# A hybrid decoder trunk on one core: the order of the mixer stage rewritten (C's norm inside the input projection, output projection C, D, B, A, joined squares)

## The chip, the core and the metric

The kernel runs on one core of one Trainium2 chip. The metric is the device time of one execution in microseconds (us). The core has TensorE (PE in the rows; PEld is its weight load, which overlaps it), VectorE (DVE), ScalarE (ACT), GpSimd (POOL) and SyncE (SP), which here only starts transfers. Each engine works through its own instructions in program order and waits on semaphores for the others.

## What is computed

Two layers, each of three steps on the same 320 tokens (256 of a prompt, 64 of eight samples), 1024 channels:

```python
x = LN(alpha*x + 1/2*(1+g1)*SwiGLU1(mod1(x)))
x = LN(alpha*x + (1+g2)*W_out[A|B|C|D](mod2(x)))   # the mixers
x = LN(alpha*x + 1/2*(1+g3)*SwiGLU2(mod3(x)))
u, v, xb, gate_b, gate_c, hc, glu_a, glu_g = split(modulate(x, sh2, sc2) @ w_in[l])
ya = gelu(u) * (W_s @ layer_norm(gelu(v)) + b_s)            # A: 4 heads of 64 channels
yb = (causal means of 2, 4, 8, 16 of xb - xb) @ pool_w * s  # B
yc = gate_b * conv3(gate_c * hc)                            # C
yd = silu(layer_norm(conv31(glu_a * sigmoid(glu_g)) + b))   # D
mix = rms_norm_groups([ya|yb|yc|yd]) @ w_out[l]
```

The shift, scale and gate of every step come from a projection of the sequence's condition ("ada" below), whose matmuls and small operations are spread over the whole kernel. The rms norm is taken over each of the four groups of 256 channels by itself, and the output projection needs the normed group of the rows of W_out that it multiplies.

## The kernel before

**Tiles.** Activations stand transposed: a tile is 128 channels x 320 tokens, so x is eight tiles and each of A, B, C, D two. Weights come through SP's queue as raw tiles of 128 x 2048 fp32; each half (128 x 1024) is one *split*: ACT copies it to `whi` (L229, a rounded copy), DVE takes `wlo = raw - whi` (L237). Activations are split the same way, into `xhi/xlo` and, for the mixers' outputs, `mh` (ACT, L845) and `ml` (DVE, L851). A product of one 128 x 128 weight tile with a 128 x 320 tile is then three matmuls (hi*hi, hi*lo, lo*hi). `acc3` (L664 to L666) does one product at a time; `kouter` (L673, L674, L678) takes one input row k and feeds several output tiles at once.

**The mixer stage**, once in each layer, is `mix_body`. Its parts in order:

- `zchunk` multiplies the eight rows of x into five output tiles `zcm0` to `zcm4`: the two halves of D's `glu_a`, the two of its `glu_g`, and the first half of B's input. D's gate (`sigmoid`, product) follows, and then its 31-tap causal convolution: the first tap of each half on ACT (`dtap0`), the other thirty on DVE, `dtap` (L915), one instruction for one tap of one half, 60 in a layer. They are laid between the other work by `hook`, a function that is called as each weight tile of a projection is taken and issues taps while a credit is left (0.465 a tap).
- the list `MIX_SEQ` gives the order of everything else by short names; the program issues each name's instructions on whatever engines they run on, and that order is the order of every engine. `hc`, `gc`, `gb` are C's three projections for one half, `xb`, `up`, `val` those of B and A. `mean` first empties the list of taps and then computes D's channel mean (`cmn`, L1108, PE); `sub` subtracts it (L1112, DVE), `sq4` squares (ACT, L826), `stat4` sums the squares over channels (PE, `rr`, L534), `pow4` makes the inverse root (DVE L1123, POOL L1124), `bc4` spreads it over the partitions (PE, L603), `norm` and `swish` finish D. Groups 2 (C), 3 (D), 1 (B) and 0 (A) then go through `sq`, `stat`, `pow`, `bc`, `mul` (DVE L834), `hi` and `lo` the same way. `cconv`, `ctaps`, `cgate` are C's product, taps and gate on DVE. `pool` and `poolmm` are B's running sums (DVE) and its small projection (`pb`, PE L966), `sgu` and `sgate` A's mixing over tokens (`pm`, PE L1027 and L1029) and its gate. `ada` is a piece of the ada projection (`adp`, L461).
- `ko0` to `ko5` multiply the first six rows of the output projection (groups in the order `WO_GROUPS`, two rows each) into the first `CH` = 5 output tiles `wo`; the loop over `WO_ORDER` then finishes these five with the last two rows (6 matmuls each) and computes the other three whole (24 matmuls each). After each tile comes `evac`: gate, add to x (DVE L816, ACT L817, DVE L819), and `acc_add`, which keeps the running sums S and Q of x and x*x for the LN (DVE L558, L559). `TAIL_SPLIT` says after which tiles a weight split of the next stage is made.
- the LN (`ln_finish`): the last sums (L574, L575), their total over channels on PE (`nbm`, `rbm`, L534), and so on to the first product of the next stage (`zch` after the mixers).

The PSUM tiles come from a pool of six banks handed out in turn and one of two for the small statistics.

```python
MIX_SEQ = """
    pool0 hc0 xb1 up0 val vstat up1 gc0 gb0 vnorm cconv0 gc1 hc1 gb1 mean cconv1 sub sq4 ada6 ctaps0 ctaps1 cgate0
    cgate1 stat4 pow4 vgain ada2 sq2 bc4 norm swish stat2 sq3 sgu pow2 pool1 ada2 stat3 bc2 pow3 poolmm mul2 hi2
    sq1 sgate bc3 lo2 sq0 ada2 stat1 mul3 hi3 pow1 ko0 stat0 lo3 pow0 bc1 mul1 ko1 hi1 lo1 step step bc0 mul0 hi0
    ada18 ko2 lo0 ko3 ko4 ko5
"""
```

Of the kernel before, what the change touches and what calls it, by code (L numbers as in the profile page):

```python
# [61 lines left out]
WO_ORDER = (0, 1, 3, 2, 6, 5, 4, 7)  # L62
WO_GROUPS = (2, 1, 3, 0)
TAIL_SPLIT = (1, (0, 0, 0, 0, 2, 1, 0, 0))
# [7 lines left out]
""".split()
MIX_OPS = [(w.rstrip("0123456789"), int("0" + w.lstrip("abcdefghijklmnopqrstuvwxyz"))) for w in MIX_SEQ]
# [4 lines left out]
            "mul": 0.9, "lo": 0.8, "sub": 0.8, "norm": 0.8}  # L78
# [214 lines left out]
class Kern:  # L293
# [389 lines left out]
    def zchunk(self, nm, n, mid=None):  # L683
# [173 lines left out]
    def mix_body(self, l, gb, G, late):  # L857
# [32 lines left out]
        banks = self.zchunk(nm, CH, sig_table)  # L890
# [26 lines left out]
        taps = [dtap(i, j) for i in range(1, 31) for j in range(2)]  # L917
# [11 lines left out]


# [89 lines left out]
        def spatial():  # L1020
            for jj in range(2):
                pt = self.mm(f"pm{l}{jj}")
                for hh in range(2):
                    h = 2 * jj + hh
                    o = pt[64 * hh:64 * hh + 64]
                    for cc in range(2):
# [395 lines left out]
```

## Time and profile before

| | before |
|---|---|
| runs | 1307.23, 1304.6, 1293.9 us (median 1304.6) |
| the profiled execution's own time | 1306.28 us |
| its span, first to last instruction | 1304.5 us |
| PE busy | 1268.1 us (97%) |
| DVE, ACT, POOL busy | 730.3, 555.6, 23.3 us |
| matmuls | 9310 |
| mean granted TensorE clock | 0.977 |
| mixer stage, layer 0: first `zcm` to first `zch` | 286.91 to 422.03 us |
| mixer stage, layer 1 | 915.34 to 1056.93 us |

A row of the timeline has the start, the duration, the engine, the line and the operation, out<-in, how often it stands in a row, and in brackets the engine's idle time before it and who ended it. A row of several instructions gives the time from the first's start to the last's end. On PE, one fp32 matmul is counted as two or more passes, and a duration is that of one instruction in the pipeline: neighbouring ones overlap, so the step from start to start is what a matmul costs. PEclk is the granted share of the 2.4 GHz clock, 0.50 meaning 1.2 GHz.

### The profile page before, as it was taken

How to read it: one execution, taken by the hardware profiler on the slowest of the kernel's cores; microseconds unless marked ns; L12 is line 12 of the kernel's file. 1: busy time of each engine (PE TensorE's matmuls, PEld its weight loads, DVE VectorE, ACT ScalarE, POOL GpSimd, SP SyncE). 2: the span in 40 equal slices, each digit the busy share in tenths (PEclk: the TensorE clock that was granted, in tenths of full speed). 3: DMA queues.
4: the chain of work that ended last, by engine and by line, in shares of the span. 5: the costliest groups of instructions: out<-in, count | busy, mean ns of one | idle time of the engine just before them, and what ended most of it. 6: DMA issues, size and time to landing. Idle time of an engine off the chain costs nothing.

```text
span 1304.5 us, 22088 instructions
## 1 busy us (share of the span) xinstructions
PE 1268.1 (97%) x9310; PEld 1215.6 (93%) x9310; DVE 730.3 (56%) x1321; ACT 555.6 (43%) x872; POOL 23.3 (2%) x39
## 2 busy tenths in 40 slices
PE   6999999999999999999999999999997999999996
PEld 4999999999888999999999999999995989999996
DVE  4644444468966744454575444445896575444444
ACT  3643333347344634343345343333742446343432
POOL 0000000000010000000000000000000000000000
PEclk9999999999979999999999999999996999999998
DMA  9765556568849654544465546554864794444301
GB/s 375 282 236 209 211 194 248 201 215 245 303 162 120 264 204 137 205 149 162 162 218 206 181 172 216 183 206 161 227 251 162 73 262 163 134 157 157 134 1 41
DMA packets 63747, 247.45 MB, mean 190 GB/s; under 512 B 31072, under 2 KB 33632, under 8 KB 34464
## 3 DMA queue, kind: packets, MB, share of 16 engines
q1 hardware_dynamic: 58912, 245.11, 56.0%
q8 instruction: 73, 1.20, 0.4%
q10 hardware_dynamic: 4736, 0.93, 0.4%
q14 instruction: 26, 0.21, 0.1%
HBM read 243.45 MB, written 2.57 MB: 189 GB/s over the span
## 4 chain that ended last, share of the span: by engine, by line
PE 72%; issue 19%; DVE 5%; DMA 2%; ACT 1%; POOL 0%; SPq 0%; POOLq 0%; ACTq 0%; DVEq 0%
PE of L664 4%; PE of L666 4%; PE adp L461 4%; PE of L665 4%; PE uf L664 4%; PE uf L666 4%; PE uf L665 4%; PE gf L664 3%; PE gf L666 3%; PE gf L665 3%; PE oh L665 2%; PE oh L666 2%; PE oh L664 2%; DVE aD L915 2%; PE uh L664 2%
## 5 line engine op out<-in xcount | busy, mean ns | idle before, releaser
L237 DVE TENSOR_TENSOR wlo<-raw,whi 128x1024 fp32r<-128x1024 f32 x312 | 373.7, 1226 | 135.6 <-ACT whi L229 134.9
L229 ACT CAST whi<-raw 128x1024 fp32r<-128x1024 f32 x312 | 315.1, 1045 | 26.2 <-issue 8.4
L664 PE MATMUL of<-hhf,whi 128*128 128x320 f32 x352 | 109.6, 311 | 0.0
L666 PE MATMUL of<-hhf,wlo 128*128 128x320 f32 x352 | 109.1, 310 | 0.0
L665 PE MATMUL of<-hlf,whi 128*128 128x320 f32 x352 | 109.1, 310 | 0.0
L665 PE MATMUL oh<-hlh,whi 128*128 128x320 f32 x352 | 108.6, 309 | 0.0
L666 PE MATMUL oh<-hhh,wlo 128*128 128x320 f32 x352 | 108.6, 309 | 0.0
L664 PE MATMUL oh<-hhh,whi 128*128 128x320 f32 x352 | 108.6, 309 | 0.0
L664 PE MATMUL uf<-xhif,whi 128*128 128x320 f32 x320 | 99.5, 311 | 0.0
L664 PE MATMUL uh<-xhih,whi 128*128 128x320 f32 x320 | 99.1, 310 | 0.0
L665 PE MATMUL uh<-xloh,whi 128*128 128x320 f32 x320 | 99.0, 309 | 0.0
L666 PE MATMUL uf<-xhif,wlo 128*128 128x320 f32 x320 | 99.0, 309 | 0.0
L666 PE MATMUL uh<-xhih,wlo 128*128 128x320 f32 x320 | 99.0, 309 | 0.0
L665 PE MATMUL uf<-xlof,whi 128*128 128x320 f32 x320 | 99.0, 309 | 0.0
L664 PE MATMUL gf<-xhif,whi 128*128 128x320 f32 x304 | 94.6, 311 | 0.0
L664 PE MATMUL gh<-xhih,whi 128*128 128x320 f32 x304 | 94.2, 310 | 0.0
L666 PE MATMUL gf<-xhif,wlo 128*128 128x320 f32 x304 | 94.0, 309 | 0.0
L666 PE MATMUL gh<-xhih,wlo 128*128 128x320 f32 x304 | 94.0, 309 | 0.0
L665 PE MATMUL gf<-xlof,whi 128*128 128x320 f32 x304 | 94.0, 309 | 0.0
L665 PE MATMUL gh<-xloh,whi 128*128 128x320 f32 x304 | 94.0, 309 | 0.0
L767 ACT CAST hhf<-sgf 128x320 fp32r<-128x320 f32 x44 | 20.2, 459 | 134.3 <-DVE sgf L764 134.3
L767 ACT CAST hhh<-sgh 128x320 fp32r<-128x320 f32 x44 | 20.2, 459 | 134.3 <-DVE sgh L764 134.3
(332 smaller groups left out, 2818.0 us busy)
## 6 DMA issues: line engine op xcount, KB each, us to landing
raw<-in_w_main SPq DMA_DIRECT2D x156, 1024.0 KB, 4.9
raw<-in_w_ada SPq DMA_DIRECT2D x72, 1024.0 KB, 6.6
out_yT<-x SPq DMA_DIRECT2D x8, 160.0 KB, 1.8
xt<-in_x SPq DMA_DIRECT2D x2, 512.0 KB
wsT<-in_wsT SPq DMA_DIRECT2D x2, 256.0 KB
sgln<-in_sgln SPq DMA_DIRECT2D x2, 256.0 KB, 4.8
cD<-in_pre_d SPq DMA_DIRECT2D x4, 120.0 KB, 9.3
out_o_ds<-cD ACTq DMA_DIRECT2D x4, 120.0 KB, 14.0
```

The source lines that it names most:

```text
L229: kk.nc.scalar.copy(hi, raw)
L237: self.kk.nc.vector.tensor_tensor(lo, raw, hi, op=ALU.subtract)
L461: nc.tensor.matmul(ps[32 * g:32 * g + 32, 0:w], self.cs[:, k, :], wt[:, h, g * w:(g + 1) * w], start=(k == 0), stop=(k == NK - 1))
L664: mm(ps, hi, xh, start=first, stop=False)
L665: mm(ps, hi, xl, start=False, stop=False)
L666: mm(ps, lo, xh, start=False, stop=last)
L767: nc.scalar.copy(hi, sg)
L915: return lambda: V.scalar_tensor_tensor(o, cD[j][:, :, i:i + 8], wv, o, op0=ALU.mult, op1=ALU.add)
```

## The change

Everything changed lies in the mixer stage; the arithmetic is the same apart from the order of some sums.

- `MIX_SEQ` is rewritten. C's six projections come first, in the order gc, hc, gb, and C's product, taps, gate, squares, statistics, `mul`, `hi` and `lo` follow while the projections of B and A (`xb`, `val`, `up`) still run. `ko0` and `ko1`, C's two rows of the output projection, stand ahead of `mean`.
- `WO_GROUPS` goes from C, B, D, A to C, D, B, A. Four tiles, not five, are begun by rows (`CHO`). In the last loop, tiles that were begun by rows (6 matmuls left) and tiles computed whole (24 matmuls) take turns, and the weight splits are laid after other tiles (`TAIL_SPLIT`).
- `qa` adds the two squared tiles of a group on DVE, so that the sum over channels takes half the matmuls; `mean` adds the two halves of D first, likewise.
- In `zchunk` the last rows of x go tile by tile (`MIX_LAST`), the two tiles of D's half 0 first; D's half 0 is gated, and four of its taps are issued, ahead of half 1.
- B's second running sum (`pool1`) is cut into pieces (`p2`, `p3`, ...) laid between the steps of D's norm; `vgain` comes after `norm`; `w` makes one weight split; the two heads of a `pm` tile take turns.
- PSUM tiles are handed out in turn, so that the new order gives other banks: the program now has `pb00`, `pb01` and `pm01` in one bank and `adp32` and `pm00` in another, one after the other, where all six had banks of their own.

```diff
-WO_ORDER = (0, 1, 3, 2, 6, 5, 4, 7)
-WO_GROUPS = (2, 1, 3, 0)
-TAIL_SPLIT = (1, (0, 0, 0, 0, 2, 1, 0, 0))
+WO_ORDER = (0, 4, 1, 5, 2, 6, 3, 7)
+WO_GROUPS = (2, 3, 1, 0)
+CHO = 4
+TAIL_SPLIT = (1, (0, 1, 0, 1, 0, 1, 0, 0))
...
+    gc0 hc0 pool0 gb0 cconv0 gc1 hc1 ctaps0 gb1 cconv1 ctaps1 xb1 cgate0 cgate1 sq2 val qa2 stat2 pow2 up0 bc2 mul2 hi2
+    lo2 vstat up1 vnorm ko0 t99 ko1 mean p2 sub sq4 p3 ada4 qa4 stat4 p2 pow4 p4 ada4 bc4 step p9 norm swish poolmm
+    step vgain sq3 step sgu qa3 stat3 sq1 pow3 sgate bc3 mul3 hi3 qa1 stat1 lo3 pow1 sq0 ko2 bc1 mul1 hi1 qa0 lo1 stat0 ko3
+    pow0 w ko4 bc0 mul0 hi0 w ko5 lo0 w
...
+MIX_HEAD = (12, 13, 14, 15, 4)
+MIX_LAST = [(k, m) for k in (4, 5) for m in range(4)] + [(k, m) for ms in ((0, 2), (1, 3)) for m in ms for k in (6, 7)] \
+    + [(k, 4) for k in range(4, 8)]
...
-        self.qlast = (self.d0 if m == 1 else self.accS, d, self.square(d, f"{self.nm}{m}"))
+        self.qlast = (self.d0 if self.first else self.accS, d, self.square(d, f"{self.nm}{m}"))
+        self.first = False
...
+            if last and k >= 4:
+                if k == 4 and mid:
+                    mid()
+                cut = next(i for i, (kk, _) in enumerate(last) if kk > 5)
+                for kk, m in last[:cut] if k == 4 else last[cut:]:
+                    self.acc3(banks[m], st.tile(), self.xk(kk), False, kk == NK - 1)
+                continue
...
-        taps = [dtap(i, j) for i in range(1, 31) for j in range(2)]
+        taps = [dtap(i, 0) for i in range(1, 5)] + [dtap(i + 4 * (1 - j), j) for i in range(1, 27) for j in range(2)]
+        taps += [dtap(i, 1) for i in range(27, 31)]
...
+        dgate(0)
+        dtap0(0)
+        taps_(4)
+        dgate(1)
+        dtap0(1)
...
-                banks.extend(self.mm(f"wo{l}{m}") for m in range(CH))
+                banks.extend(self.mm(f"wo{l}{m}") for m in range(CHO))
...
-            for j in range(2):
-                nc.tensor.matmul(rr[5][:, 0:N], self.o256, aD[j], start=(j == 0), stop=(j == 1))
+            s = mp.tile([P, N], F32, tag="rsq", bufs=4, name=f"sD{l}")
+            V.tensor_tensor(s, aD[0], aD[1], op=ALU.add)
+            nc.tensor.matmul(rr[5][:, 0:N], self.o256, s, start=True, stop=True)
...
+        def qa(grp):
+            a, b = qs[grp]
+            V.tensor_tensor(a, a, b, op=ALU.add)
+            qs[grp] = [a]
...
+        def ahead_one(_):
+            st.split_until(min(st.nsplit + 1, ahead(st.u) + 1))
...
-            po = banks[m] if m < CH else self.mm(f"wo{l}{m}")
-            for k in range(6 if m < CH else 0, NK):
+            po = banks[m] if m < CHO else self.mm(f"wo{l}{m}")
+            for k in range(6 if m < CHO else 0, NK):
```

Three places in the order of the instructions follow. A row is line, operation, out<-in and shape; the numbers behind names tell buffers apart.

**First place: DVE ahead of D's mean, layer 0.** Before, from the last taps (`aD`) on, with the split `wlo85`, C's product `ec`, the subtraction of the mean (L1112) and C's taps (`yC`):

```order
L915 SCALAR_TENSOR_TENSOR aD00_3154<-cD00_2901,par_79,aD00_3154 128x320
L915 SCALAR_TENSOR_TENSOR aD01_3155<-cD01_2905,par_79,aD01_3155 128x320
L237 TENSOR_TENSOR wlo85_3714<-raw74_3537,whi85_3713 128x1024
L1065 TENSOR_TENSOR ec01_2920<-hc01_3676,gcs01_3674 128x256
L1066 TENSOR_TENSOR esc01_2921<-hc01_3676,gcs01_3674 128x8x8
L1112 TENSOR_TENSOR aD00_3154<-aD00_3154,cmn0_3750 128x320
L1112 TENSOR_TENSOR aD01_3155<-aD01_3155,cmn0_3750 128x320
L1080 SCALAR_TENSOR_TENSOR yC00_3610<-ec00_2912,par_79,yC00_3610 128x256
```

Of the change, from C's joined squares (L1153) to the sum of D's halves (L1141) that the mean reads:

```order
L242 TENSOR_TENSOR wlo83_3616<-raw71_3350,whi83_3615 128x1024
L1153 TENSOR_TENSOR sqrm020_3547<-sqrm020_3547,sqrm021_3549 128x320
L1162 TENSOR_SCALAR rv02_3681<-rr02_3677 128x3
...
L847 SCALAR_TENSOR_TENSOR yC00_3338<-yC00_3338,par_79,rr02_3677 128x320
...
L864 TENSOR_TENSOR ml021_3730<-yC01_3479,mh021_3729 128x320
...
L242 TENSOR_TENSOR wlo85_3747<-raw74_3513,whi85_3746 128x1024
...
L926 SCALAR_TENSOR_TENSOR aD00_3154<-cD00_2901,par_79,aD00_3154 128x320
...
L1141 TENSOR_TENSOR sD0_3819<-aD00_3154,aD01_3155 128x320
```

C's taps, gate, join, `mul` and `ml` and the split `wlo85` now all stand ahead of the last taps of D; eleven taps are left behind the join.

**Second place: PE from D's mean on, layer 0.** Before (`adp` is the ada projection, `rr` the statistics, here of D):

```order
L666 MATMUL gb01_3712<-xhim07_3068,wlo81_3525 128x320
L1108 MATMUL cmn0_3750<-aD00_3154,o256_101 128x320
L1108 MATMUL cmn0_3750<-aD01_3155,o256_101 128x320
L461 MATMUL adp32_3764<-raw75_3539,cs_78 32x256 x8
L461 MATMUL adp32_3764<-raw75_3541,cs_78 32x256 x8
```

Of the change, up to B's projection `pb` and A's mixing `pm`:

```order
L684 MATMUL wo03_3785<-ml021_3730,whi82_3554 128x320
L1142 MATMUL cmn0_3818<-sD0_3819,o256_101 128x320
L466 MATMUL adp32_3838<-raw75_3515,cs_78 32x256 x8
...
L539 MATMUL rr04_3860<-o256_101,sqrm040_3831 128x1 x3
...
L609 MATMUL rr04_3860<-ident_80,rv04_3866 128x128 x2
...
L995 MATMUL pb00_3906<-pl00_3285,pw0_2058 128x320
L995 MATMUL pb01_3909<-pl01_3822,pw0_2058 128x320
L489 MATMUL adp32_3838<-sel_81,adev14_3896 128x36 x2
```

The mean stood behind the last projection, `gb01`; now it stands behind C's two rows of the output projection, and D's statistics take one row of three where six matmuls stood.

**Third place: DVE at the end of the stage, layer 0.** Before, from the last split `wlo93` to the last tile (`evsm07`):

```order
L237 TENSOR_TENSOR wlo93_4258<-raw82_3783,whi93_4257 128x1024
L816 TENSOR_TENSOR evsm05_4263<-wo05_4232,ada0_107 128x64
L558 TENSOR_TENSOR Sm0_4114<-Sm0_4114,x6_353 128x320
L559 TENSOR_TENSOR Qm0_4115<-Qm0_4115,sqm06_4230 128x320
L819 TENSOR_TENSOR x5_239<-x5_239,evsm05_4263 128x320
L816 TENSOR_TENSOR evsm04_4277<-wo04_3965,ada0_107 128x64
L558 TENSOR_TENSOR Sm0_4114<-Sm0_4114,x5_239 128x320
L559 TENSOR_TENSOR Qm0_4115<-Qm0_4115,sqm05_4269 128x320
L819 TENSOR_TENSOR x4_237<-x4_237,evsm04_4277 128x320
L558 TENSOR_TENSOR Sm0_4114<-Sm0_4114,x4_237 128x320
L559 TENSOR_TENSOR Qm0_4115<-Qm0_4115,sqm04_4283 128x320
L811 TENSOR_TENSOR evsm07_4310<-wo07_4285,ada0_107 128x64
```

Of the change, the same stretch:

```order
L242 TENSOR_TENSOR wlo92_4245<-raw82_3857,whi92_4244 128x1024
L829 TENSOR_TENSOR evsm06_4248<-wo06_4219,ada0_107 128x64
L564 TENSOR_TENSOR Sm0_4080<-Sm0_4080,x2_233 128x320
L565 TENSOR_TENSOR Qm0_4081<-Qm0_4081,sqm02_4217 128x320
L832 TENSOR_TENSOR x6_353<-x6_353,evsm06_4248 128x320
L829 TENSOR_TENSOR evsm03_4262<-wo03_3785,ada0_107 128x64
L564 TENSOR_TENSOR Sm0_4080<-Sm0_4080,x6_353 128x320
L565 TENSOR_TENSOR Qm0_4081<-Qm0_4081,sqm06_4254 128x320
L832 TENSOR_TENSOR x3_235<-x3_235,evsm03_4262 128x320
L564 TENSOR_TENSOR Sm0_4080<-Sm0_4080,x3_235 128x320
L565 TENSOR_TENSOR Qm0_4081<-Qm0_4081,sqm03_4268 128x320
L824 TENSOR_TENSOR evsm07_4295<-wo07_4270,ada0_107 128x64
```

The split `wlo93` has left the stretch (it now stands in the LN, behind the subtraction of the mean from three tiles), and the tile before the last is a short one again, but one that the 24 matmuls of `wo06` precede.

## Rows read from the trace of the kernel before

**Rows 1.** Waits of PE: us in total, times, longest us.

```profile
PE nbm L534 <- DVE Sm L574: 5.9, 2, 3.0
```

**Rows 2.** Timeline of PE, layer 0, from D's mean to the first output row.

```profile
354.40 1.24 PE L1108 MATMUL cmn<-aD,o 128*128 128x320 f32 x4
355.56 2.80 PE L461 MATMUL adp<-raw,cs 128*32 128x256 f32 x48
358.29 1.50 PE L534 MATMUL rr<-o,sqrm 128*128 128x1 f32 x12
...
361.08 0.88 PE L603 MATMUL rr<-ident,rv 128*128 128x128 f32 x6 [0.29 <-POOL rv L1124]
...
363.18 0.65 PE L1027 MATMUL pm<-wsT,v 128*64 128x128 f32 x4
...
368.49 2.70 PE L534 MATMUL rr<-o,sqrm 128*128 128x1 f32 x12
371.05 1.52 PE L603 MATMUL rr<-ident,rv 128*128 128x128 f32 x6
372.37 2.45 PE L966 MATMUL pb<-pl,pw 128*128 128x320 f32 x4
...
378.00 0.39 PE L673 MATMUL wo<-mh,whi 128*128 128x320 f32 x1
```

**Rows 3.** Timeline of PE, layer 1, the same places and the last output row.

```profile
984.17 2.50 PE L1108 MATMUL cmn<-aD,o 128*128 128x320 f32 x4 [5.75 <-DVE aD L915]
...
1012.35 0.61 PE L673 MATMUL wo<-mh,whi 128*128 128x320 f32 x1
...
1045.23 0.31 PE L666 MATMUL wo<-mh,wlo 128*128 128x320 f32 x1
```

**Rows 4.** Timeline of DVE, layer 0, around D's mean.

```profile
352.89 0.56 DVE L915 SCALAR_TENSOR_TENSOR aD<-cD,par,aD 128x320 f32<-128x320 f32 x1
353.35 1.23 DVE L237 TENSOR_TENSOR wlo<-raw,whi 128x1024 fp32r<-128x1024 f32 x1
354.49 0.43 DVE L1065 TENSOR_TENSOR ec<-hc,gcs 128x256 f32<-128x256 f32 x1
...
355.67 0.89 DVE L1112 TENSOR_TENSOR aD<-aD,cmn 128x320 f32<-128x320 f32 x2 [0.62 <-PE cmn L1108]
356.47 0.48 DVE L1080 SCALAR_TENSOR_TENSOR yC<-ec,par,yC 128x256 f32<-128x256 f32 x1
...
358.84 0.89 DVE L1083 TENSOR_TENSOR yC<-yC,gbs 128x320 f32<-128x320 f32 x2
...
372.68 1.01 DVE L834 SCALAR_TENSOR_TENSOR yC<-yC,par,rr 128x320 f32<-128x320 f32 x2 [1.29 <-PE rr L603]
```

**Rows 5.** Timeline, PE of an FFN's LN, then PE and DVE of layer 0's mixers' end.

```profile
281.50 0.83 PE L534 MATMUL nbf<-o,Sf 128*128 128x1 f32 x6
...
286.91 0.41 PE L673 MATMUL zcm<-xhim,whi 128*128 128x320 f32 x1
...
406.95 0.31 PE L664 MATMUL wo<-mh,whi 128*128 128x320 f32 x1
...
410.32 0.31 PE L666 MATMUL wo<-mh,wlo 128*128 128x320 f32 x1
...
413.69 0.22 DVE L811 TENSOR_TENSOR evsm<-wo,ada 128x64 f32<-128x64 f32 x1
...
415.02 0.83 PE L534 MATMUL nbm<-o,Sm 128*128 128x1 f32 x6 [2.95 <-DVE Sm L574]
...
422.03 0.41 PE L673 MATMUL zch<-xhih,whi 128*128 128x320 f32 x1
```

**Rows 6.** Windows: us, busy of PE, PEld, DVE, ACT, POOL, then PEclk, DMA share, GB/s.

```profile
365.00:375.00 10.00, 10.00 (x40) 8.32 (x40) 4.69 (x18) 0.68 (x2) 0.85 (x1) 0.50 0.46 194
416.00:419.00 3.00, 3.00 (x23) 2.43 (x26) 1.46 (x7) 0.00 (x0) 0.85 (x1) 0.54 0.78 116
997.00:1016.00 19.00, 18.48 (x76) 16.16 (x75) 9.92 (x30) 6.10 (x14) 2.66 (x3) 0.50 0.21 87
```

More of the change, by code (lines that the diff above doesn't have):

```diff
@@ L77 @@
 DVE_COST = {"pool": 3.5, "vstat": 1.3, "vnorm": 0.1, "cconv": 0.5, "ctaps": 1.2, "cgate": 0.4, "vgain": 2.0, "sgate": 1.0,
-            "mul": 0.9, "lo": 0.8, "sub": 0.8, "norm": 0.8}
+            "mul": 0.9, "lo": 0.8, "sub": 0.8, "norm": 0.8, "qa": 0.4}
 def _pcols():
@@ L548, in acc_add @@
         if m == 0:
-            self.d0 = d
+            self.d0, self.first = d, True
             self.nc.scalar.activation(self.accQ, d, AF.Square)
@@ L681, in xk, with zchunk @@
         return self.xhi[k], self.xlo[k]
-    def zchunk(self, nm, n, mid=None):
+    def zchunk(self, nm, n, mid=None, last=None):
         st = self.st
@@ L888, in sig_table @@
             nc.scalar.activation(t, self.mhalf[:, 0:1], AF.Sigmoid)
-        banks = self.zchunk(nm, CH, sig_table)
+        banks = self.zchunk(nm, CH, sig_table, MIX_LAST)
         ga, gg = banks[0:2], banks[2:4]
@@ L928, in mix_body, with taps_ @@
         st.hook = hook
+        def taps_(n):
+            for _ in range(min(n, len(taps))):
+                taps.pop(0)()
+                self.credit -= DVE_TAP
         def bcopy(j, px):
@@ L1022, in spatial @@
                 pt = self.mm(f"pm{l}{jj}")
[L1023 to L1026, printed above, removed]
+                hs = [(2 * jj + hh, pt[64 * hh:64 * hh + 64]) for hh in range(2)]
+                for cc in range(2):
+                    for h, o in hs:
                         nc.tensor.matmul(o[:, cc * P:(cc + 1) * P], vb[cc][:, h * 64:(h + 1) * 64],
                                          self.wsT[:, h, :], start=True, stop=True)
+                for h, o in hs:
                     nc.tensor.matmul(o[:, NP_:N], vb[2][64:128, h * 64:(h + 1) * 64],
@@ L1160, in win @@
             return go
-        def taps_(n):
-            for _ in range(min(n, len(taps))):
-                taps.pop(0)()
-                self.credit -= DVE_TAP
-        ops = {"xb": win(lambda _: bcopy(1, self.proj(self.mm(f"xb{l}1")))), "val": win(lambda _: value()), "up": win(up),
+        def ahead_one(_):
+            st.split_until(min(st.nsplit + 1, ahead(st.u) + 1))
+        ops = {"w": ahead_one, "p": pool_part, "qa": qa, "xb": win(lambda _: bcopy(1, self.proj(self.mm(f"xb{l}1")))), "val": win(lambda _: value()), "up": win(up),
                "gc": win(cgin), "hc": win(chin), "gb": win(cbin), "vstat": lambda _: v_stat(),
@@ L1277, in _mix_tiles @@
     out = []
-    for k in range(NK):
-        out += [i[k, m] for m in (12, 13, 14, 15, 4)]
+    for k in range(4):
+        out += [i[k, m] for m in MIX_HEAD]
+    out += [i[k, MIX_HEAD[m]] for k, m in MIX_LAST]
     at = {"xb": 4, "val": 2, "up": 0, "gc": 8, "hc": 10, "gb": 6}
@@ L1286, in _mix_tiles @@
     for k in ks[:6]:
-        out += [o[k, m] for m in range(CH)]
+        out += [o[k, m] for m in range(CHO)]
     for m in WO_ORDER:
-        out += [o[k, m] for k in (ks[6:] if m < CH else ks)]
+        out += [o[k, m] for k in (ks[6:] if m < CHO else ks)]
     return out
```

44 lines of the change are left out of this document (23 added, 21 removed).

## The prediction, made before the changed kernel ran

> **What bounds the kernel now.** I read the waits first: PE is busy nearly all the time, and two waits of PE in the mixer stage stand out. The LN after the mixers waits for DVE's last sum in both layers, 5.9 us together [rows 1], and D's mean waits in layer 1 for the last tap, 5.75 us [rows 3]. Then I read PE's timeline from the mean to the first row of the output projection: 354.40 to 378.00, so 23.6 us in layer 0 [rows 2], and 984.17 to 1012.35, so 28.2 us in layer 1 [rows 3]. There PE is "busy", but with small pieces that follow the chain of D's norm, and the clock is low for a good part of it: 0.50 from 365 to 375 and from 997 to 1016 [rows 6]. The same small pieces show the price: twelve passes of a statistic take 1.50 us at one level and 2.70 at the other, spreading it 0.88 and 1.52 [rows 2]. The third view is the end of the stage: the last `wo` matmul starts at 410.32, but DVE begins the last tile's evacuation at 413.69, and `nbm` waits 2.95 us [rows 5]. So the mixer stage has three stretches that the change can move: until the mean, mean to first row of D, and the tail. Everything before and after it is unchanged, matmul for matmul.
>
> Clock, from these rows: after the 5.75 us without PE work in layer 1 the mean's four passes took 2.50 us, against 1.24 in layer 0, where PE came to it busy [rows 2, 3]; and 0.54 was granted behind the LN's wait of 2.95 [rows 5, 6].
>
> **Term 1, the mean comes later.** DVE's 60 taps set the mean. Before, the last tap of layer 0 is done at 353.4, with a split behind it [rows 4], and PE is just through with its projections at 354.4. After, DVE has ahead of the mean what it did behind it: C's taps 2.37 (eight from 356.47 to 358.84), C's gate 0.89, the second product about 0.5, `mul` 1.01, `ml` 0.9, the split 1.2 [rows 4], and two new adds, C's join and the sum of D's halves, 0.45 each by the subtraction's 0.89 for two [rows 4]. Less overlap between neighbours, that is 7.4. DVE also waits now: behind the join it needs PE's statistic (three matmuls, half of 1.50) and then, in front of `mul`, the spread root, which on PE stands behind a whole projection (24 x 0.147 = 3.5; the step 0.147 is 3.37 us over 23 steps, from 406.95 to 410.32 [rows 5]). With the root's 1.29 (358.29 + 1.50 to 361.08 [rows 2]) running beside it, and 2.9 us of taps and a split to do meanwhile, that leaves about 3.5 us of waiting in layer 0, hi and lo included. The mean then comes at 353.4 + 7.4 + 3.5 = 364.3, +10.0. PE itself would be there at about 362.7: it gets to C's statistic at 346.8 (354.4 less two projections of 3.5 and 0.5 of ada), waits for the join until 350.0, and then has the statistic 0.75, ada 0.5, two projections and 24 row matmuls (3 x 3.5) and the spread 0.88. In layer 1 DVE is the late one already, so it hardly waits for PE: 984.2 + 7.8 = 992.0. D's half 0 beginning 2.6 us earlier buys little, as DVE then still waits for half 1. Sum: **+10.0 and +7.8**. Bounds: if DVE doesn't wait for PE, +7 in layer 0; if the 3.2 us that PE waits for the join lower the clock for the next 24 matmuls (0.147 becomes 0.265 by the ratio 2.70 to 1.50), +2.8.
>
> **Term 2, from the mean to D's first row.** 24 row matmuls (3.5 us), C's statistic, spread, `mul`, `hi`, `lo` and taps are gone from here. What is left is one chain. In us from the mean at full clock: mean 0.6 (half of 1.24); subtraction, squares (passes of 0.45) to 2.1; DVE's pieces of B's sums 1.1 and the join to 3.2; statistic 0.75, to 4.0; root 1.3; the spread behind 32 ada matmuls (2.80 x 32/48 = 1.9) from 5.9 to 6.7; norm and swish to 8.6. Then the shared banks: `pb01` must wait until ACT, behind the swish, has read `pb00`, and ACT's second read stands ahead of D's squares: 0.5 + 0.6 (a quarter of 2.45 twice, at the higher clock) + 0.5, squares 0.85, to 11.2. `pm00`, `pm01` (about 0.85 a head pair, 0.65 for its four large passes [rows 2]) and the statistic to 13.1; A's gate on DVE (2.0, before `mul`) to 15.3; half of `mul` 0.5, `hi` 0.4 and semaphores: **16.7**. With statistics at 1.35, spreads at 1.52 and the mean at 1.25, the values of the lower clock [rows 2, 3], it is 19.9, and up to 22 in layer 1, where PE has idled about 5 us ahead of the mean. Before, the clock fell in this stretch [rows 6], and the stretch is as thin as it was. I take values between, nearer to the lower clock for layer 1: 18.5 and 20.5, so **-5.1 and -7.7**.
>
> **Term 3, D's first row to the last `wo` matmul.** Before: 378.00 to 410.6, 32.6 us [rows 2, 5], and 33.2 in layer 1 (1012.35 to 1045.5 [rows 3]). After: 48 + 24 + 96 = 168 matmuls of 0.147 are 24.7, spreads and a statistic 2.1; and two waits: B's statistic chain delays A's squares' join by 1.7 behind DVE's `mul` and `ml`, and A's `ml` stands behind a split whose `whi` ACT makes only after `hi`: 2.2. Together 30.7; with the first row's twelve matmuls at 0.265, 32.2; taken 31.5: **-1.1 and -1.7**.
>
> **Term 4, the tail.** With short and long tiles in turns a pair takes PE 30 x 0.147 = 4.4 us, while DVE has two evacuations with their sums (1.35 each) and at most one split: 3.9. DVE is free when the last tile ends, and the 2.95 us go. With no wait the clock has less reason to fall: an FFN's LN needs 5.4 us from first statistic to next product, this one 7.0 [rows 5], with 0.54 granted in it [rows 6]. Of these 1.6 the split moved into the LN's chain takes back up to 0.6. So **-4.0** each; bounds -2.95 (clock falls all the same) and -4.5.
>
> By the Trainium skill's "TensorE: Matmul & The Clock Gate", section "HAM oscillation — how this bites in real kernels", a gap in which TensorE waits sends it back to the low clock and the next matmuls start slow; rows 3 and 6 agree (2.50 against 1.24 behind 5.75 us of idling). By it the change buys nothing at the mean, as it keeps that wait in layer 1 and puts one of 3.2 us ahead of C's statistic in layer 0; this is the second rival's case.
>
> **Sum.** Layer 0: 10.0 - 5.1 - 1.1 - 4.0 = -0.2. Layer 1: 7.8 - 7.7 - 1.7 - 4.0 = -5.6. Together -5.8. Against the profiled execution's own 1306.28 that is 1300.5; the median of the runs shown is 1.7 lower, 1304.6, which gives 1298.8. **1299 us.** The joined squares and fewer statistics are in terms 2 and 3; the pairing of `pm`'s heads I cost at nothing (PE isn't late there, A's gate behind it is).
>
> **The rivals.** *The clock stays high* (2.4 GHz) through D's chain, since it is shorter and has ada matmuls between: term 2 is 16.7, term 3 30.7, term 4 -4.5. Layer 0: 10.0 - 6.9 - 1.9 = +1.2; layer 1: 7.8 - 11.5 - 2.5 = -6.2; less 9.0: -14.0, **1290.6**. For it: the chain loses C's pieces, which stood in the slow part. Against: the row 997 to 1016 [rows 6] behind just such a wait. Chance 0.22.
>
> *The clock stays low*, the other side: the idling ahead of the mean, or ahead of C's statistic, drops it to 1.2 GHz, and the thin chain does not bring it back before `ko5` in either layer. It decides if the 48 row matmuls of D and B run at 0.265 rather than 0.147: 48 x 0.118 = 5.7 a layer, of which 1.35 is in the 32.2 above. Layer 0 with all upper values: 10.0 + 2.8 - 3.7 + 0.4 = +9.5; layer 1: 7.8 - 6.2 - 0.2 = +1.4; 8.7 for the rows; tail -5.9: +13.7, **1318**. For it: 19 us at 0.50 in layer 1 before [rows 6]. Against: before, the output rows brought the clock back within a few us. Chance 0.08.
>
> *The tail gains nothing*, because DVE comes late again, through the split in the turns or A's late `ml`: +8, **1307**. Against: DVE's 3.9 us of work in 4.4. Chance 0.15.
>
> **How the numbers follow.** My forecast has 0.55. Its own range, by the bounds of terms 2 to 4, is 1293 to 1309 (upper values 9.5 + 1.4 - 5.9 = +5.0). The 8 in 10 reach into the first rival and take in the third: 1288 to 1311. A measurement of this kernel tells about 1% from no change, the runs of before lie 1% apart. Faster by over 1% (under 1291.6) is most of the first rival and the low end of mine: 0.23; slower by over 1% (over 1317.6) is the second: 0.07; the rest 0.70.
>
> **What would show it.** In the changed profile: the mean at about 364 and 992, behind waits of DVE's sum; first D row 18 to 21 us later; `pb01` behind ACT's `pl`; a wait at A's first row behind `ml`; no wait of `nbm` for the last sum, and an LN of 6 us. The mean earlier than 360, or a chain under 16 us, would prove terms 1 or 2 wrong; a wait of `nbm` over 1 us term 4.

## The result, and the profile after

| | before | after |
|---|---|---|
| median of the runs beside each other | 1301.3 us (4 runs) | 1334.0 us (4 runs, 1332.7 to 1336.96) |
| ratio, 95% interval | | 1.0266 [1.0232, 1.0300] |
| span of the profiled execution | 1304.5 | 1335.0 |
| PE busy, matmuls | 1268.1, 9310 | 1268.4, 9246 |
| DVE busy | 730.3 | 737.3 |
| both mixer stages, first `zcm` to first `zch` | 276.7 | 309.3 |
| PE idle in them | 13.6 | 43.6 |
| in them, time at 1.2 GHz (added up from windows of 1 us) | 47.8 | 85.3 |

The change costs 33 us, where I had forecast a gain of 6. Both mixer stages together are 32.5 us longer, and PE idles 30 us more in them. There are 64 fewer matmuls, yet PE is busy as long, since more of its work runs at the lower clock. By an estimate from [rows 2], where twelve passes of a statistic take 1.50 us, 64 passes are 8 us, and the lower clock has cost about as much; the larger part of the loss is the idling.

The waits of PE in the changed kernel (us in total, times, longest), those of the mixer stages; before there were 5.9 for `nbm` [rows 1], 5.75 for the mean [rows 3] and under 2 beside them:

```profile
PE cmn L1142 <- DVE sD L1141: 10.9, 2, 7.3
PE rr L539 <- DVE sqrm L1153: 8.6, 5, 2.4
PE wo L671 <- DVE ml L864: 4.5, 2, 2.2
PE adp L489 <- ACT adev L485: 4.0, 3, 2.3
PE pb L995 <- ACT pl L998: 4.0, 2, 2.0
PE nbm L539 <- DVE Sm L580: 3.7, 1, 3.7
PE rr L609 <- POOL rv L1163: 2.4, 2, 1.2
PE nbm L539 <- issue: 2.2, 1, 2.2
PE nbm L609 <- DVE vm L588: 2.1, 1, 2.1
```

No single wait carries the loss. Only those at the mean, at `nbm`, at a statistic (1.3 us then, for ACT's squares) and at the root (`rv`, 0.6 us then) were there before.

The timeline of PE in layer 0 from the mean on, to be held against [rows 2]:

```profile
366.10 1.14 PE L1142 MATMUL cmn<-sD,o 128*128 128x320 f32 x2 [3.59 <-DVE sD L1141]
367.16 3.23 PE L466 MATMUL adp<-raw,cs 128*32 128x256 f32 x32
370.32 0.83 PE L539 MATMUL rr<-o,sqrm 128*128 128x1 f32 x6
...
373.67 0.76 PE L995 MATMUL pb<-pl,pw 128*128 128x320 f32 x2
376.44 1.24 PE L995 MATMUL pb<-pl,pw 128*128 128x320 f32 x2 [2.01 <-ACT pl L998]
...
381.69 1.44 PE L539 MATMUL rr<-o,sqrm 128*128 128x1 f32 x6
384.31 1.54 PE L609 MATMUL rr<-ident,rv 128*128 128x128 f32 x6 [1.18 <-POOL rv L1163]
387.34 1.44 PE L539 MATMUL rr<-o,sqrm 128*128 128x1 f32 x6 [1.50 <-DVE sqrm L1153]
```

The statistic takes 0.83 us at 370 and 1.44 from 381 on: behind the wait of `pb` the granted clock falls, as windows show (the row of 14 us has 0.52; the last 19 us, dense with `wo`, have 1.00; the LN has 0.58, against 0.54 in [rows 6]):

```profile
376.00:390.00 14.00, 10.49 (x53) 8.78 (x54) 5.93 (x18) 3.99 (x10) 1.70 (x2) 0.52 0.39 160
405.00:424.00 19.00, 18.27 (x131) 17.88 (x135) 13.45 (x29) 8.44 (x15) 0.00 (x0) 1.00 1.07 122
428.00:436.00 8.00, 7.41 (x52) 5.76 (x56) 4.56 (x12) 1.41 (x2) 0.85 (x1) 0.58 0.99 152
```

By the four terms of the prediction (us, each layer before -> after; before, the first output row behind the mean is C's, and the second and third stretch are cut there):

| stretch | layer 0 | layer 1 | forecast |
|---|---|---|---|
| first `zcm` to mean | 67.5 -> 80.9 (+13.4) | 68.8 -> 83.3 (+14.5) | +10.0, +7.8 |
| mean to D's first row | 23.6 -> 22.5 (-1.1) | 28.2 -> 22.9 (-5.3) | -5.1, -7.7 |
| D's first row to last `wo` | 32.6 -> 34.8 (+2.2) | 33.2 -> 37.8 (+4.6) | -1.1, -1.7 |
| last `wo` to next stage | 11.4 -> 13.4 (+2.0) | 11.4 -> 13.7 (+2.3) | -4.0, -4.0 |

All eight came out worse than I had put them.

### The profile page after: what moved, and what is told of

The parts are those of the page before. It is cut to its first block, busy times and chain, and to the rows that moved or that the text cites. A ratio compares the mean times of both kernels' runs of the same rounds, so it can differ in the third digit from the quotient of the medians.

```text
span 1335.0 us, 21963 instructions
## 1 busy us (share of the span) xinstructions
PE 1268.4 (95%) x9246; PEld 1213.9 (91%) x9246; DVE 737.3 (55%) x1333; ACT 556.0 (42%) x872; POOL 25.2 (2%) x39
## 4 chain that ended last, share of the span: by engine, by line
PE 65%; issue 19%; DVE 11%; ACT 3%; DMA 1%; POOL 0%; another core or an unknown queue 0%; POOLq 0%; ACTq 0%; SPq 0%; DVEq 0%
PE of L670 4%; PE of L672 4%; PE of L671 4%; PE adp L466 4%; PE uf L670 4%; PE uf L672 4%; PE uf L671 4%; PE gf L670 3%; PE gf L672 3%; PE gf L671 3%; DVE aD L926 3%; DVE wlo L242 3%; PE oh L670 2%; PE oh L671 2%; PE oh L672 2%
```

## The experiments

Sixteen kernels. Ratios are against the kernel before on the same chip, with their 95% intervals; between kernels that ran on different chips they are the safer comparison. "The stage" is the mixer stage. In the diffs `...` stands for lines left out, and lines of the list are joined and shortened to the names that change.

### Which part of the change

**seq_before**: the changed kernel with the old list and group order.

```diff
-WO_GROUPS = (2, 3, 1, 0)
+WO_GROUPS = (2, 1, 3, 0)
-    gc0 hc0 pool0 gb0 cconv0 gc1 hc1 ctaps0 gb1 cconv1 ctaps1 xb1 cgate0 cgate1 sq2 val qa2 stat2 pow2 up0 bc2 mul2 hi2
...
+    pool0 hc0 xb1 up0 val vstat up1 gc0 gb0 vnorm cconv0 gc1 hc1 gb1 mean cconv1 sub sq4 ada6 ctaps0 ctaps1 cgate0
...
-                    st.hold = True
```

> The changed kernel with the old list MIX_SEQ and the old group order C, B, D, A; kept are the joined mean, D's first rows early, the four row tiles, the alternating end and its splits. The statistics of the groups take two squared tiles again, as the old list has no join. Theory S (the new sequence costs the time: C's norm on DVE ahead of D's last taps makes the mean late by about 14 us a layer, of which 6 are new idling of PE): the stretch up to the mean and the chain are as before, about 1301 plus what the new end costs, so 1303 to 1311. Theory T (the new end of the stage and its splits cost the time, last row of D's chain to LN: +4 us in layer 0, +7 in layer 1 in the changed kernel's trace, and the rest is clock lost through it): stays above 1318.

1303.0 us, 1.0002 [0.9972, 1.0032]. So the list, with its group order and the joins and splits that it calls, makes the 33 us; early D, the new end, the joined mean and the pairing of heads run like the kernel before.

**tail_before** and **tail_alone**: the end of the stage undone in the changed kernel (its diff), and done alone in the kernel before (the reverse, with `CHO` = 4).

```diff
-WO_ORDER = (0, 4, 1, 5, 2, 6, 3, 7)
+WO_ORDER = (0, 1, 3, 2, 6, 5, 4, 7)
-TAIL_SPLIT = (1, (0, 1, 0, 1, 0, 1, 0, 0))
+TAIL_SPLIT = (1, (0, 0, 0, 0, 2, 1, 0, 0))
```

> The changed kernel with the old order and splits at the end: the four row tiles finished first (0, 1, 3, 2), then the four whole tiles (6, 5, 4, 7), two splits after the first whole tile and one after the second. Theory S: only the end improves, 2 us a layer at the LN's wait and up to 2 in front of it: 1326 to 1331. Theory T: more than half of the 33 us comes back, under 1318. If the old end was the worse one, as I had forecast, it gets slower: 1340.

> The kernel before with only the new end: four tiles begun by rows instead of five, short and long tiles in turns, the new splits. Theory S: the wait of nbm stays or grows by 1 us and the rest is as before: 1301 to 1307. Theory T: 1315 or more. My forecast of the end (no wait of nbm): 1293.

1337.2 us, 1.0255 [1.0209, 1.0300], and 1301.8 us, 1.0005 [0.9968, 1.0042]. The end neither costs nor gains. In tail_alone the wait of `nbm` did shrink, as I had forecast, from 2.95 us to 1.7 in each layer, and the stretch from the last `wo` to the next stage from 11.4 to 10.1 and 10.4; the time doesn't show it. This settled against theory T.

### Within the list: where D's mean, C's rows and C's norm stand

**mean_first**: D's last taps and mean ahead of C's `mul`, rows behind the mean.

```diff
-up0 bc2 mul2 hi2 lo2 vstat up1 vnorm ko0 t99 ko1 mean p2 sub sq4 p3 ada4 qa4 stat4 p2 pow4 p4 ada4 bc4 step p9
+up0 bc2 up1 mean mul2 hi2 sub sq4 lo2 ko0 qa4 ko1 stat4 p2 pow4 vstat vnorm p3 ada8 bc4 step p9 p9
```

> The changed kernel with D's last taps and the mean moved ahead of C's mul, lo and A's statistics on DVE, and ko0, ko1 behind the mean on PE, into D's chain. Theory S with DVE's order as its mechanism: the mean comes at 359 instead of 366 in layer 0 and 6 to 8 us earlier in layer 1, PE's idling ahead of it (3.6 and 7.3) goes, ko0 and ko1 fill the chain: 1314 to 1322. Rival (the two PSUM banks left and the thin chain set the time, wherever the mean stands): the chain gets longer by as much, 1330 or more.

1331.1 us, 1.0204 [1.0146, 1.0262]: the rival. The mean did come 6.3 and 9.0 us earlier in the stage, and the stretch from it to the last `wo` grew by 5.0 and 4.2, with `pb`'s wait grown to 3.5 us in each layer. So the mean's lateness was not the whole matter. It gains 3 us over the change by the medians and 8 by the ratios, whose intervals overlap.

**rows_late**: only `ko0` and `ko1` move, behind A's mixing.

```diff
-vnorm ko0 t99 ko1 mean
+vnorm t99 mean
...
-sgu qa3 stat3 sq1 pow3 sgate bc3 mul3
+sgu qa3 stat3 ko0 sq1 pow3 sgate bc3 ko1 mul3
```

> The changed kernel with ko0 and ko1 moved from ahead of the mean to behind A's mixing (ko0 after D's statistic, ko1 after its spread). Nothing else moves. Theory B (with four output tiles begun ahead of the mean only two PSUM banks are left for pb, pm and adp, and PE has no rows to fill the waits behind D's norm): pb01's wait of 2.0 us and pm's of 0.4 go and the 24 matmuls lie in waits of D's last steps; PE idles 3.5 us more ahead of the mean, which DVE sets: 1322 to 1328. Rival (the mean's lateness alone counts, which is DVE's): 1332 to 1340.

1319.7 us, 1.0145 [1.0111, 1.0180]: 14 us back, the most that one move within the list gave, though PE idles 3.5 us more ahead of the mean in each layer. The stretch from the mean to the last `wo` is 50.3 and 50.7 us instead of 57.4 and 60.6, and the same window as above has 1.00 of the clock:

```profile
376.00:390.00 14.00, 11.52 (x96) 10.71 (x96) 9.36 (x27) 6.45 (x15) 2.01 (x3) 1.00 0.42 173
```

**c_norm_late**: as rows_late, and C's squares, statistic, `mul`, `hi`, `lo` behind the mean.

```diff
-cgate1 sq2 val qa2 stat2 pow2 up0 bc2 mul2 hi2 lo2 vstat
+cgate1 val up0 vstat
...
-sub sq4 p3 ada4 qa4 stat4 p2 pow4 p4 ada4 bc4 step p9 norm swish poolmm
+sub sq4 sq2 p3 ada4 qa4 stat4 qa2 p2 pow4 stat2 p4 pow2 ada4 bc4 step p9 norm swish bc2 mul2 hi2 lo2 poolmm
```

> As the kernel with ko0 and ko1 late, and C's squares, statistics, mul, hi and lo also go from ahead of the mean into D's chain, where they stood before; C's projections, taps and gate stay early. Theory H (the place of C's norm is the cost: before, its steps filled the waits of D's chain for nothing, and ahead of the mean each is paid in full): mean 5 to 7 us earlier than in the changed kernel, chain no longer: 1308 to 1316. Rival (the taps and the gate ahead of the mean are the cost): the same as with the rows late, within 3 us.

1321.8 us, 1.0170 [1.0132, 1.0207]: the same as rows_late. The mean came 5.0 and 7.0 us earlier and the chain behind it took 8.7 and 6.3 longer. Theory H fell: where C's norm stands, by itself, moves the time from one side of the mean to the other.

### Why the early rows cost: banks or fill

**two_tiles**: the rows stay ahead of the mean, for two output tiles instead of four.

```diff
-CHO = 4
+CHO = 2
```

> The changed kernel with two output tiles begun by rows instead of four: ko0 and ko1 still stand ahead of the mean, with half the matmuls, and four PSUM banks are free for pb, pm and adp. Theory B, banks (the shared banks set the wait behind D's norm): pb01's wait of 2.0 us and the waits that follow from it go, D's squares come 2 to 3 us earlier: 1322 to 1328, most of what the kernel with the rows late gained. Theory F, fill (that kernel gained because 24 matmuls came into the thin stretch behind D's norm): the shared-bank wait goes too, but now fewer rows stand there, so the time stays at 1332 to 1340.

1330.1 us, 1.0218 [1.0177, 1.0260], between the two ranges; the interval overlaps that of the change. The wait of `pb` is gone and `pm` runs at the high clock, but behind it nothing wide stands between the steps of the norms, the waits open up, and the clock falls all the same (layer 0):

```profile
378.75 0.83 PE L539 MATMUL rr<-o,sqrm 128*128 128x1 f32 x6
380.76 1.54 PE L609 MATMUL rr<-ident,rv 128*128 128x128 f32 x6 [1.18 <-POOL rv L1163]
383.80 1.44 PE L539 MATMUL rr<-o,sqrm 128*128 128x1 f32 x6 [1.50 <-DVE sqrm L1153]
```

This edit is not of one thing only: with two tiles `ko2` to `ko5` are half as long too, and the end has more whole tiles (15.8 us from the last `wo` in layer 0, against 13.4).

**banks_early** and **banks_held**: rows_late with the four output tiles handed out in `mean`, not in `ko`; in the second only, the last two lines, a one-column matmul into each, make it hold its bank.

```diff
+            banks.extend(self.mm(f"wo{l}{m}") for m in range(CHO))
+            for b in banks:
+                nc.tensor.matmul(b[:, 0:1], self.o256, self.o256[:, 0:1], start=True, stop=True)
```

> The kernel with the rows late, but the four PSUM banks of the output tiles are handed out at the mean, as in the changed kernel; the matmuls of ko0 and ko1 stay behind D's statistic. So pb, pm and adp share two banks again, and the rows still fill the thin stretch. If the banks are the price of the early rows: back to 1328 to 1334. If the rows' place itself is (24 wide matmuls behind D's norm instead of ahead of the mean): 1319 to 1324, with the wait of pb01 on ACT back at 2 us a layer.

> The kernel with the rows late, and at the mean four small matmuls (one column each, overwritten by ko0 later) into the four output tiles, so that these hold their PSUM banks from there on and pb, pm and adp share two, bank for bank as in the changed kernel. In the kernel called banks_early the banks went to pb, pm and adp all the same, as a bank is held only from its first matmul on, so that it was the kernel with the rows late once more. If the shared banks are the price of the early rows: 1328 to 1334, with pb01's wait of 2 us for ACT back in both layers. If the rows' place is: 1319 to 1324, two waits of 2 us at most.

banks_early: 1319.3 us, 1.0133 [1.0098, 1.0168]; its banks are those of rows_late, tile for tile, so it says only that rows_late repeats: its window from 376 to 390 has 1.00 of the clock too. Its stretch from the mean to the last `wo` is 54.7 us in layer 0, where rows_late has 50.3, so a single execution's stretch is good to some 4 us. banks_held: 1331.2 us, 1.0256 [1.0214, 1.0298]. With the rows where rows_late has them and the banks as the change has them, 11.5 of the 14 us are lost again (by the ratios, 14 of 16). The five tiles named under The change share two banks in it, as there. The timelines of PE in layer 0, first rows_late, then banks_held:

```profile
374.35 1.29 PE L995 MATMUL pb<-pl,pw 128*128 128x320 f32 x4
375.49 0.53 PE L489 MATMUL adp<-sel,adev 128*128 128x36 f32 x4
376.83 0.78 PE L1055 MATMUL pm<-wsT,v 128*64 128x128 f32 x8 [0.82 <-DVE v L1043]
...
378.79 0.83 PE L539 MATMUL rr<-o,sqrm 128*128 128x1 f32 x6
```

```profile
377.02 1.33 PE L995 MATMUL pb<-pl,pw 128*128 128x320 f32 x2 [2.01 <-ACT pl L998]
378.15 0.90 PE L489 MATMUL adp<-sel,adev 128*128 128x36 f32 x4
379.45 1.12 PE L1055 MATMUL pm<-wsT,v 128*64 128x128 f32 x8 [0.40 <-DVE ada L498]
...
382.38 1.44 PE L539 MATMUL rr<-o,sqrm 128*128 128x1 f32 x6
```

Waits of 2.4 us, where rows_late has one of 0.8, have become 3.8 by the statistic (96.8 us into the stage, against 93.0), since what follows `pb` runs at the lower clock; both stages spend 64.8 us at 1.2 GHz, rows_late 44.4. By the last `wo` it is 6.2 and 5.9 us. So the early rows cost through their banks; two_tiles suggests that free banks alone help little where the rows are missing behind D's norm. In both kernels the clock falls there.

### The joined squares

**no_join** and **join_alone**: the joins undone in the changed kernel (`qa` does nothing, the mean takes two halves again: the lines with -), and `qa` put into the old list ahead of each `stat`.

```diff
-            V.tensor_tensor(a, a, b, op=ALU.add)
-            V.tensor_tensor(s, aD[0], aD[1], op=ALU.add)
...
-sq4 ada6 ctaps0 ctaps1
+sq4 ada6 ctaps0 qa4 ctaps1
-swish stat2
+swish qa2 stat2
```

> The changed kernel with the joins undone: the statistics read two squared tiles (six matmuls) and the mean two halves, without the adds on DVE. Theory J (the join puts DVE, which is still busy with mul and lo of the group before, into each group's chain: the changed trace shows PE waiting 1.5 and 1.6 us for the joined squares of B and A, and 1.9 us of DVE's own waiting behind C's): these waits go, 3 to 5 us a layer: 1324 to 1328. Rival (the matmuls saved are worth as much, 0.75 us each at the high clock and 1.35 at the low one, five in a layer): 1334 to 1339.

> The kernel before with only the joins of the squares: qa ahead of each group's statistic, three matmuls instead of six; the mean keeps its two halves. If the join puts DVE's queue in front of the statistic (theory J): 1305 to 1312, PE waiting 1 to 2 us for joined squares. If the matmuls saved are worth more (three of 0.24 us at the low clock, four times a layer): 1294 to 1299. As much: 1300 to 1304.

no_join: 1328.4 us, 1.0219 [1.0161, 1.0277], its interval overlaps that of the change, though PE's 8.6 us of waiting for joined squares are gone. join_alone: 1310.7 us, 1.0070 [1.0041, 1.0098], 9 us slower. The squares stand in DVE's queue now (timeline of PE, layer 0):

```profile
361.99 0.93 PE L603 MATMUL rr<-ident,rv 128*128 128x128 f32 x6 [2.85 <-POOL rv L1129]
364.30 1.44 PE L534 MATMUL rr<-o,sqrm 128*128 128x1 f32 x6 [1.38 <-DVE sqrm L1119]
```

The spread starts 8.6 us behind the mean (353.41 there), before 6.7 (361.08 behind 354.40 [rows 2]), although its statistic takes 0.83 instead of 1.50, and the clock fell behind the wait: 68.2 us at 1.2 GHz against 47.8. So the join costs in the old list. In the new one not even the direction is shown.

### Putting it right, and looking for a gain

**waits_out**: rows_late, no joins, and A's `ml` ahead of a weight split. **all_out**: the same with the mean first. **all_out_w**: all_out with `ml` behind the split again.

```diff
-pow0 w ko4 bc0 mul0 hi0 w ko5 lo0 w
+pow0 w ko4 bc0 mul0 hi0 lo0 w ko5 w
```

> The kernel with the rows late, without the joins (statistics of two squared tiles, mean of two halves), and with A's ml ahead of the weight split that it stood behind. What was left in that kernel's chain were waits of 1.6 us for A's joined squares and 2.2 us for A's ml in each layer. If such waits count in full: 1319.7 less 7.7, 1310 to 1314. If the chain only shifts (the next wait takes their place): 1316 to 1321.

> As the last kernel, and D's last taps and mean ahead of C's mul and lo as well. C's projections, taps, gate and squares stay early. The kernel with the mean first had the mean 6 us (layer 0) and 9 us (layer 1) earlier and lost it again in a chain on two banks; with the rows late the banks are there. If these four (rows ahead of the mean, joins, the split ahead of ml, C's norm ahead of the last taps) are the whole cost: 1299 to 1306. If C's taps and gate ahead of D's mean cost by themselves: 1307 to 1314.

> The kernel with everything out, with A's ml behind the weight split again, as the change has it. In that kernel's trace the wait of 2.2 us for ml was gone, but nbm waited 5.4 us for DVE instead of 2 to 4, and PE 2 us in the next stage. If the split's work only moved to the end of the stage: the same time or less, 1307 to 1313. If ml ahead of the split is a gain: 1315 to 1317.

1320.2 us, 1.0132 [1.0082, 1.0182]; 1311.8 us, 1.0084 [1.0056, 1.0112]; 1313.6 us, 1.0093 [1.0068, 1.0118]. Taking the waits of 1.6 and 2.2 us out gave nothing: PE's waits for `ml` and for A's joined squares are gone, and these two came in waits_out (us in total, times, longest):

```profile
PE nbm L539 <- DVE Sm L580: 10.8, 2, 5.4
PE zch L679 <- ACT xhih L646: 2.2, 1, 2.2
```

Moving the split behind `ml` moved its work to the end: all_out_w, where PE waits for `ml` again, is as fast, a little above the range put for that. The mean first gives 8 us by the medians with the banks free (6 by the ratios, whose intervals overlap); with them shared it gave 3 and 8, so whether it needs free banks isn't shown. all_out's two stages are as long as before (277.5 against 276.7): 12.5 us less from the mean to the last `wo`, 6.1 more ahead of it, 7.2 more behind it. PE's 4.3 us of waiting for `xhih` lie past the stage's end. The spans of the two profiled executions are 6.0 us apart (1310.5 and 1304.5), and these two make 5.1 of it; by the medians all_out is 9 to 11 us slower. all_out lies in the range that I had put for C's taps and gate costing by themselves, but its stages don't show such a cost. So 9 to 11 of the 33 us stay open, and so does why the splits end up at the end.

**pool0_late** and **hi_early** looked for a kernel faster than both: the kernel before with the new end and B's first running sum behind the mean; and with the new end and each split's ACT copy ahead of the tile's squares.

```diff
-pow2 pool1 ada2
+pow2 pool0 pool1 ada2
...
-            split(TAIL_SPLIT[1][i])
+            st.split_lo(pend)
             self.evac(po, Gt, xs[m], m)
+            if i + 1 < NK and TAIL_SPLIT[1][i + 1]:
+                pend = st.split_hi(min(st.nsplit + 1, ahead(st.u) + 1))
             if m < NK - 1:
```

> The kernel before with the new end alone, and B's first running sum (2.8 us of DVE) moved from ahead of the taps to ahead of the second one, behind the mean, where DVE idled 3.9 us. If DVE's work ahead of the mean is what counts, layer 1's wait of 5.75 us for the last tap becomes 3, layer 0 has no such wait and gains nothing, and the clock may stay up longer behind it: 1294 to 1299. If the chain behind the mean takes it back: 1301 to 1304.

> The kernel before with the new end, and each weight split's ACT copy between a tile's gate and its squares, its DVE half a tile later, so that DVE doesn't wait 1.48 us for ACT at each split. If that wait makes DVE late on the last tile: nbm's wait of 1.7 to 1.8 us goes, and the LN takes 1 us less: 1294 to 1299. If DVE is late through its ping-pong with ACT alone: 1300 to 1303.

1302.7 us, 1.0036 [1.0004, 1.0069], and 1302.6 us, 1.0000 [0.9970, 1.0029]. In both the wait that was aimed at shrank (layer 1's mean from 5.75 to 4.1; `nbm`'s for the last sum to none) and another came (the chain behind the mean; 3.9 us for the next stage's first `xhih`). None of the sixteen beats the kernel before.

## Why the prediction was wrong

The stages came out 32.5 us longer where I had put them 5.8 shorter: a miss of 38 us, of which terms 1 to 4 have 10.1, 6.4, 9.6 and 12.3 (both layers, from the table). In terms 1 to 3 the steps that failed are mainly waits between the engines that I left out or counted in one layer only, and the clock behind them; in term 4 it is DVE's time for two tiles and a split, and how late A's norm leaves DVE.

**What bounds it** was read in part: the loss lies in the mixer stages, and the three stretches that I named moved. The fourth, from D's first row to the last `wo`, I had not counted among those that the change can move, and it grew by 6.8 us in all.

**Term 1, +10.0 and +7.8, was +13.4 and +14.5.** The work that moves ahead of the mean was nearly right: in layer 1 DVE is busy 69.9 us from the stage's start to the mean, before 61.9, so 8.0 against my 7.4. What failed is "DVE is the late one already, so it hardly waits for PE", said of layer 1. It waited for the statistic 1.44 us and for the spread 3.69 (timeline of DVE, layer 1), 5.1 of the 6.7 us that are missing:

```profile
992.33 0.16 DVE L1162 TENSOR_SCALAR rv<-rr 128x3 f32<-128x3 f32 x1 [1.44 <-PE rr L539]
999.16 1.01 DVE L847 SCALAR_TENSOR_TENSOR yC<-yC,par,rr 128x320 f32<-128x320 f32 x2 [3.69 <-PE rr L609]
```

The spread stands on PE behind a projection, and that projection ran at the lower clock, 6.4 us instead of 3.8, behind PE's wait of 2.4 us for C's join (the granted clock is 0.51 from 991 to 998). I knew that order and charged it in layer 0 alone. There DVE's waits for the two came out as forecast, 3.4 us against 3.5 (timeline of DVE, layer 0):

```profile
350.76 0.16 DVE L1162 TENSOR_SCALAR rv<-rr 128x3 f32<-128x3 f32 x1 [1.89 <-PE rr L539]
355.45 1.01 DVE L847 SCALAR_TENSOR_TENSOR yC<-yC,par,rr 128x320 f32<-128x320 f32 x2 [1.46 <-PE rr L609]
```

The 3.4 us that are missing in layer 0 are work, 70.1 us up to the mean against 61.2 up to the last tap before, so 8.9 for my 7.4, and some 2 us of smaller waits of DVE. I also missed a wait of PE in layer 0: ACT makes C's first tap, which now waits 6.4 us for DVE's product, and the ada copy is queued behind it, for which PE waits 2.3; the next projection then takes 5.3 us instead of 3.7. So PE, which I had put ahead of C's join, begins the statistic 1.1 us behind it (348.87 to 349.99), and more than that DVE can't have lost by it. The timeline of ACT, and of PE:

```profile
323.65 0.51 ACT L1101 ACTIVATE yC<-ec,par 128x256 f32<-128x256 f32 x1 [6.39 <-DVE ec L1094]
...
324.31 0.35 ACT L485 COPY adev<-adp 128x256 f32<-128x256 f32 x1
```

```profile
324.71 0.64 PE L489 MATMUL adp<-sel,adev 128*128 128x36 f32 x4 [2.33 <-ACT adev L485]
325.18 0.39 PE L670 MATMUL hc<-xhim,whi 128*128 128x320 f32 x1
```

The moved step's queue on ACT was left out, though I had followed it on DVE and PE.

**Term 2, 18.5 and 20.5, was 22.5 and 22.9.** The chain and its banks were seen: `pb01` waits where I put it, 2.0 us. Two steps failed. I laid the wait into a chain priced between the two clocks, and the lower clock came with the wait itself (0.63 of the clock from 376 to 390 in banks_held, 1.00 in rows_late): held alone (banks_held) the banks cost 11.5 us, not the 2.4 a layer of their waits. And I let D's first row start behind `hi`; on PE, B's statistic stands ahead of it, which waits 1.5 us for B's join behind D's `mul` and takes 1.44: 2.9 of the 4 us in layer 0.

**Term 3, 31.5, was 34.8 and 37.8.** The two waits of 1.7 and 2.2 us are there as forecast (1.59 and 2.23). The missing part is the clock: I had allowed one row, 12 matmuls, at the lower level as a bound. In layer 0 it reaches into 36: the first row takes 3.55 us, where rows_late's takes 2.0, and the next two 5.3, there 3.8. In layer 1 these two take 6.1, and from 1055.9 to 1059.3, behind the wait for `ml`, 0.50 was granted once more.

**Term 4, -4.0, was +2.0 and +2.3.** The step "DVE's 3.9 us of work in 4.4" failed. At each split DVE waits 1.5 us for ACT's copy, which stands behind a tile's squares, and two tiles with a split take it 5.5 us. The timeline of DVE, layer 0, and PE's wait:

```profile
401.57 1.01 DVE L847 SCALAR_TENSOR_TENSOR gu<-gu,par,rr 128x320 f32<-128x320 f32 x2 [4.47 <-PE rr L609]
...
416.85 1.23 DVE L242 TENSOR_TENSOR wlo<-raw,whi 128x1024 fp32r<-128x1024 f32 x1 [1.47 <-ACT whi L234]
418.00 0.22 DVE L829 TENSOR_TENSOR evsm<-wo,ada 128x64 f32<-128x64 f32 x1
...
423.48 0.22 DVE L829 TENSOR_TENSOR evsm<-wo,ada 128x64 f32<-128x64 f32 x1
...
427.27 0.22 DVE L824 TENSOR_TENSOR evsm<-wo,ada 128x64 f32<-128x64 f32 x1
...
428.60 1.44 PE L539 MATMUL nbm<-o,Sm 128*128 128x1 f32 x6 [3.71 <-DVE Sm L580]
```

The last product starts at 423.15, and DVE begins the last tile 4.1 us later. By itself the new end does shorten the tail, but only by 1.0 to 1.3 us (tail_alone). seq_before has the same end and the same order of DVE from A's `mul` to the last tile, the splits included, and its tails are 10.1 and 10.0 us. DVE takes 26.4 us for this there, 0.6 of them a wait for PE, and 25.7 in the changed kernel (layer 0, from 401.57). PE, though, has less left to do: its last product starts 24.3 us behind A's `mul` in seq_before and 21.6 in the changed kernel (24.3 and 23.1 in layer 1). So the new list ends A's norm late against PE's matmuls, and what DVE still has to do behind them is the tail.

**The joined squares** I put into terms 2 and 3 as a gain of matmuls. join_alone shows the opposite for the old list: the add costs more in DVE's order than the three matmuls on PE.

**The rivals.** The second, clock low for long, was the nearest: 85 us at 1.2 GHz, and 1318 was my price. It was still short by 16 us, since it took the waits as forecast. Its sum has a slip: for term 3 it adds 0.4 and takes off 0.2, where the bound of 32.2 gives -0.4 and -1.0, so that its price is 1317 and the upper end of my range 1308. By the Trainium skill's "TensorE: Matmul & The Clock Gate", section "HAM oscillation — how this bites in real kernels", which I had cited, a gap in which TensorE waits sends it back to the lower clock. The trace agrees for the most part: slow rows stand behind the waits for the ada copy, for C's join, for the mean, for `pb` and for `nbm`, and behind that for `ml` in layer 1, though not in layer 0 (1.00 from 405 on). I had given that rival 0.08, when the order of instructions showed the new waits.

## What to carry to other kernels

Moving a step out of a chain on which TensorE waits need not gain or lose anything: with C's norm back behind the mean, the mean came 5.0 and 7.0 us earlier and the chain took 8.7 and 6.3 longer (c_norm_late). A PSUM tile that is begun early holds its bank until it is finished; count the banks that are left for the chain in between before beginning one. When a step moves, go through the queues of all engines that it issues on, ACT's too, and price a wait of PE together with the clock behind it. At the end of a stage, hold what the slower engine still has to do against what PE has left.

## What the runs showed of the hardware

Waits of TensorE of 2.0 and 0.4 us, with few and narrow matmuls around them, came with 0.63 of the clock over 14 us in banks_held, where the same stretch of rows_late, with one wait of 0.8 us, had 1.00. Six passes of a statistic and two `pm` tiles took 1.44 and 3.0 us instead of 0.83 and 1.9, and 2.4 us of waiting turned into about 6 a layer by the last `wo`.
